# Issuing the reloads of the weight buffers from GpSimd's queue instead of SyncE's in a hybrid mLSTM/HGRN2 layer

## The chip, the cores and the metric

The kernel runs on one core of a Trainium2 chip. The metric is the device time of one execution in microseconds (us), lower is better. The core has five engines that each run their own list of instructions in order: TensorE (PE: matmuls; its weight loads are shown as PEld), VectorE (DVE), ScalarE (ACT), GpSimd (POOL) and SyncE (SP), which here does nothing but start transfers (DMAs). A transfer is started by an instruction of one engine's list, is carried out by 16 DMA engines, and raises a semaphore when it has landed.

## The reference

One inference step of one decoder layer for 320 tokens: 256 of a new prompt, and 8 sequences of 8 sample tokens. All is float32, D = 2048. One input projection `proj = x @ w_in` feeds two token mixers and two merge gates. Mixer A is an mLSTM with 4 heads (keys of 256, values of 512), mixer B an HGRN2 recurrence with 8 heads (128 and 256). Then:

```python
ya = branch_a @ w_branch_a          # branch_a = norm(mLSTM(q, k, v)) * sigmoid(o)
yb = branch_b @ w_branch_b          # branch_b = norm(HGRN2(q, f, i)) * silu(g)
merged = sigmoid(gate_a) * ya + sigmoid(gate_b) * yb
x1 = layernorm(alpha * x + merged @ w_out)
y  = layernorm(alpha * x1 + square(relu(x1 @ w_up)) @ w_down)
```

Besides y, the new states of both mixers are returned (C, n, m of the mLSTM and S of HGRN2), for the prompt and for each of the 8 sample sequences.

## The kernel before

**The work on weights.** All weight matrices together are 304 tiles of 2048 x 128. A tile is multiplied in 16 steps along its 2048 rows, and each step takes three matmuls of 128 x 128 by 128 x 320: since one matmul of the fast float32 kind doesn't keep all bits, weights and tokens are split into a high and a low part (`wh`, `wl`; `xh`, `xl`), and high x high, high x low and low x high are summed in one PSUM bank. That makes 304 x 16 x 3 = 14592 matmuls, and PE runs them in the order of the tiles: for each of 4 mLSTM heads four tiles of values, two of keys, two of queries and two of merge gates; four more gate tiles; for each of 8 HGRN heads two gate tiles and the head's four; then the output gates, the branch projections, `w_out`, and four rounds of `w_up` and `w_down`.

**How weights come.** Weights move in units of half a tile: 128 x 1024 float32, 512 KB, 608 units, numbered in the order of use. A unit goes through these steps:

1. a transfer from memory into one of three raw buffers (`self.wr`, `RAW` = 3, unit u in buffer u % 3). The first six units come in pieces (`start`, at the head of the program); each later one is a *reload* (`reload`, L511 to L513);
2. ACT copies raw to `wh` (`prep`, instruction at helper line L334, shown as `wh<-wr`);
3. DVE computes raw minus `wh`, which is `wl` (`low_half`, L504, shown as `wl<-wr,wh`). With that the raw buffer is free, and `low_half` of unit u starts the `reload` of unit u + 3;
4. PE uses the pair `wh`, `wl` in 24 matmuls, and gives it back (`give`). There are three such pairs; from the `w_out` tiles on five more, carved out of a buffer `bb`.

`A` (L334), `mm` (L340) and `dma` (L343) are helpers, so nearly all of ACT's operations, of the weight matmuls and of SP's transfers show the helper's line; they are told apart by the names of their tiles.

**The heads.** What the mLSTM and HGRN heads do with their projections runs beside the weight matmuls: small matmuls on PE between those on weights (L1117, L1316, and others at L340 such as `bank<-f`), evacuations of PSUM banks on ACT (`f<-bank`), and element work on DVE. Much of it is turned or copied by round trips through memory, all issued by SP: stores of a transposed head output in small pieces (`turned`, L1311 and L1322, shown as `hT<-f`; the pieces of the sample tokens leave from a pool of two small buffers), the values of a head turned once by a store into `vtD` and a load back (`rows_to` L1010, `rows_from` L1018), copies of the sample tokens' values (`copies_to` L1069, `copies_from` L1075, `vsDm`), and the keys, written once into `kD` (L1096, eight stores per head) for use at the end. The old states C are loaded (L1349) and the new ones stored by SP as well. At the end of the kernel `m_C` reads the keys and the turned values back for the prompt's new state C, by four pairs of loads issued by GpSimd (L1197, L1198). GpSimd has else only memsets: at the start, and during the HGRN heads at L1431, L1436 (which fills a buffer after DVE has read it at L1434) and once at L428.

**What sets the order.** The program is written out by a planner in Python (`Sched`, L145 to L232) when the kernel is built. It holds one modelled clock per engine (`pe`, `act`, `dve`, `pool`, `sp`). `run_main` walks through the weight matmuls, adds 147 ns to PE's clock for each, and after each step *pumps* the chains: generators which yield requests of the form (engine, cost in ns, function). A request is issued when its modelled inputs are ready at PE's modelled time or nearly so; that puts the instruction at the end of its engine's list. Chains with a lower priority number go first, and a reload has -1, the first of all. So the order on every engine follows from modelled costs, and the chip then runs each list in order, whatever the real times. For transfers the model adds fixed times to landing: a reload's data are ready for `prep` 3200 ns after its modelled issue ends (L513), a store of turned values 5000 ns after it.

Of the kernel before, what the change touches and what calls it, by code (L numbers as in the profile page):

```python
# [295 lines left out]
class Program:  # L296
# [212 lines left out]
            self.rest_ev.t = e  # L509

    def reload(self, u, at):  # L511
        t = yield ("sp", 620, lambda: self.dma(self.wr[:, u % self.RAW, :], self.d["wt"][u]), (at,))
        self.raw_at[u] = t + 3200.0  # L513

    def run_main(self):
# [1720 lines left out]
```

## Time and profile before

| | us |
|---|---|
| median of 3 runs | 2289.7 |
| lowest and highest of these | 2287.66 and 2290.4 |
| the profiled execution, its time | 2291.95 |
| the profiled execution, its span | 2290.2 |
| TensorE's mean granted clock in it (share of full) | 0.998 |

The profiled execution is one run recorded instruction by instruction. Its span goes from the first recorded instruction to the last; the time of the execution holds 1.75 us around it. DMA moved 432.88 MB in the span, 189 GB/s, of which the hardware queue used by SP had 427.24 MB and the software queue used by GpSimd 3.15 MB.

How to read the lines: in the page's part on engines, a name is followed by its busy time, its share of the span and its number of instructions. In the part on groups, a line names the source line, the engine, the operation and output<-input by the program's names, then the count, the busy time and the mean time of one in ns, and behind the second bar the idle time just before these instructions and what ended it. In a timeline a row begins with the start and the duration in us, and a bracket holds the idle time before it and what it waited for. In a list of waits the columns are the total, the number and the longest. A queue's own row has the engine's name with a q (SPq).

### The profile page before, as it was taken

What the parts mean: (1) busy time and instruction counts of PE and PEld (TensorE: products, weight loads), DVE (VectorE), ACT (ScalarE), POOL (GpSimd) and SP (SyncE); (2) the same over time, 40 slices, a digit from 0 to 9 for tenths busy, and PEclk for the clock granted to TensorE, in tenths of its full rate; (3) what the DMA queues carried; (4) which work ended last, traced back from release to release, by engine and by line L of the source; (5) the groups of instructions that cost most, each with busy time, mean ns of one, the idle gap of its engine ahead of it and who ended that gap; (6) DMA issues with size and microseconds to landing.
All of it is one profiled execution on the core that took longest, in us unless ns stands there. A gap on an engine that the chain in (4) does not pass through costs nothing.

```text
span 2290.2 us, 39073 instructions
## 1 busy us (share of the span) xinstructions
PE 2272.9 (99%) x15546; PEld 2234.0 (98%) x15546; DVE 1425.1 (62%) x2490; ACT 1013.0 (44%) x1574; POOL 13.5 (1%) x42
## 2 busy tenths in 40 slices
PE   9999999999999999999999999999999999999998
PEld 8999889999999999999999999999999999999998
DVE  6667568788888876555655769544444444444566
ACT  5443445455555565444433547423433343334434
POOL 0000000000000000000000000000000000000000
PEclk9999999999999999999999999999999999999999
DMA  7898697676777665555555644444444444444644
GB/s 234 277 280 283 215 287 232 212 222 202 215 220 231 198 199 174 172 172 177 175 170 190 213 153 145 155 149 152 151 147 150 154 148 148 152 151 148 197 153 157
DMA packets 251167, 432.88 MB, mean 189 GB/s; under 512 B 106844, under 2 KB 146916, under 8 KB 250984
## 3 DMA queue, kind: packets, MB, share of 16 engines
q1 hardware_dynamic: 250088, 427.24, 57.7%
q0 software_dynamic: 896, 3.15, 0.5%
q8 instruction: 122, 2.00, 0.4%
q14 instruction: 61, 0.50, 0.1%
HBM read 377.30 MB, written 53.00 MB: 188 GB/s over the span
## 4 chain that ended last, share of the span: by engine, by line
PE 91%; DMA 4%; DVE 2%; ACT 1%; SPq 1%; issue 1%; ACTq 0%; DVEq 0%
PE bank L340 91%; DMA wr<-wt 3%; ACT wh L334 1%; DVE wl L504 1%; SPq L343 1%; ACT f3m L334 0%; DMA f<-xT 0%; DMA f2a<-scr 0%; DMA scr<-f 0%; DMA hT<-f 0%; DMA rx<-wt 0%; DVE rx L1378 0%; ACT f L334 0%; ACT oC L334 0%; DVE f L1007 0%
## 5 line engine op out<-in xcount | busy, mean ns | idle before, releaser
L340 PE MATMUL bank<-xh,wh 128*128 128x320 f32 x2408 | 760.3, 317 | 0.4 <-ACT wh L334 0.4
L340 PE MATMUL bank<-xh,wl 128*128 128x320 f32 x2408 | 744.1, 310 | 0.1
L340 PE MATMUL bank<-xl,wh 128*128 128x320 f32 x2408 | 741.2, 309 | 0.0
L334 ACT ACTIVATE wh<-wr 128x1024 fp32r<-128x1024 f32 (+1 forms) x432 | 453.0, 1049 | 642.5 <-PE bank L340 561.3
L504 DVE TENSOR_TENSOR wl<-wr,wh 128x1024 fp32r<-128x1024 f32 x423 | 516.9, 1222 | 333.5 <-ACT wh L334 325.4
L340 PEld LDWEIGHTS bank<-xh,wh 128*128 128x128 f32 x2408 | 453.5, 189 | 6.7 <-issue 3.9
L340 PEld LDWEIGHTS bank<-xl,wh 128*128 128x128 f32 x2408 | 453.2, 188 | 2.7
L340 PEld LDWEIGHTS bank<-xh,wl 128*128 128x128 f32 x2408 | 453.7, 189 | 0.6 <-DVE wl L504 0.6
L334 ACT ACTIVATE bb<-wr 128x1024 fp32r<-128x1024 f32 x181 | 191.9, 1061 | 356.4 <-PE bank L340 342.2
L504 DVE TENSOR_TENSOR bb<-wr,bb 128x1024 fp32r<-128x1024 f32 x179 | 219.1, 1225 | 162.3 <-ACT bb L334 162.3
L340 PE MATMUL bank<-xh,bb 128*128 128x320 f32 (+1 forms) x1280 | 284.1, 309 | 0.0
L340 PE MATMUL bank<-ra,bb 128*128 128x320 f32 x1264 | 283.4, 308 | 0.0
L340 PE MATMUL bank<-rxb,bb 128*128 128x320 f32 x1112 | 255.0, 309 | 0.0
L340 PE MATMUL bank<-ra,wh 128*128 128x320 f32 x892 | 248.9, 308 | 0.0
L340 PEld LDWEIGHTS bank<-xh,bb 128*128 128x128 f32 x1280 | 214.7, 188 | 0.0
L340 PEld LDWEIGHTS bank<-ra,bb 128*128 128x128 f32 x1264 | 210.6, 188 | 0.2
L340 PE MATMUL bank<-xl,bb 128*128 128x320 f32 (+1 forms) x640 | 197.5, 309 | 0.0
L340 PEld LDWEIGHTS bank<-rxb,bb 128*128 128x128 f32 x1112 | 188.4, 188 | 0.2
L340 PE MATMUL bank<-rxb,wl 128*128 128x320 f32 x596 | 183.7, 308 | 0.0
L340 PE MATMUL bank<-rxb,wh 128*128 128x320 f32 x596 | 183.7, 308 | 0.0
L340 PEld LDWEIGHTS bank<-ra,wh 128*128 128x128 f32 x892 | 161.4, 188 | 0.0
L340 PEld LDWEIGHTS bank<-xl,bb 128*128 128x128 f32 x640 | 120.2, 188 | 0.0
(333 smaller groups left out, 2145.3 us busy)
## 6 DMA issues: line engine op xcount, KB each, us to landing
wr<-wt SPq DMA_DIRECT2D x602, 512.0 KB
rx<-C SPq DMA_DIRECT2D x34, 256.0 KB
Cs<-rx SPq DMA_DIRECT2D x34, 256.0 KB
f<-C SPq DMA_DIRECT2D x30, 256.0 KB
Cs<-f SPq DMA_DIRECT2D x30, 256.0 KB
f<-xT SPq DMA_DIRECT2D x26, 160.0 KB
f<-S SPq DMA_DIRECT2D x8, 512.0 KB
f3h<-S SPq DMA_DIRECT2D x8, 512.0 KB
```

Source lines behind the costliest of these rows:

```text
L334: return self.nc.scalar.activation(out, in_, func, **kw)
L340: self.nc.tensor.matmul(*a, **kw)
L343: self.nc.sync.dma_start(out, in_)
L504: self.V().tensor_tensor(lo, raw, hi.bitcast(F32), ALU.subtract)
```

## The change

One line of `reload` is changed. The transfer is requested from the engine `pool` and issued by `self.nc.gpsimd.dma_start`, where it was requested from `sp` and issued by the helper `dma`, which is `self.nc.sync.dma_start`. The cost that the planner counts is 1000 in place of 620. The 602 reloads of units 6 to 607 are concerned; the transfers of the first six units, in `start`, stay on SP, and so do all transfers of the heads.

```diff
     def reload(self, u, at):
-        t = yield ("sp", 620, lambda: self.dma(self.wr[:, u % self.RAW, :], self.d["wt"][u]), (at,))
+        t = yield ("pool", 1000, lambda: self.nc.gpsimd.dma_start(self.wr[:, u % self.RAW, :], self.d["wt"][u]), (at,))
         self.raw_at[u] = t + 3200.0
```

As the planner decides with its clocks, all five lists are written anew: SP's loses the 602 reloads, GpSimd's gains them, and the order on PE, ACT and DVE differs from that of before in about the first 825 us of the program.

## The prediction

> **What bounds the kernel now.** I read the page's first line, then a table of windows, then the waits and the timelines of the windows in which TensorE stood. The columns of the windows are the stretch, its length, the busy time of PE, PEld, DVE, ACT and POOL (with counts), TensorE's granted clock, the DMA engines' busy share and GB/s.
>
> ```profile
> PE 2272.9 (99%) x15546; PEld 2234.0 (98%) x15546; DVE 1425.1 (62%) x2490; ACT 1013.0 (44%) x1574; POOL 13.5 (1%) x42
> ```
> ```profile
> 40.00:150.00 110.00, 109.83 (x749) 103.70 (x748) 69.89 (x144) 44.60 (x75) 0.00 (x0) 1.00 0.87 276
> 150.00:243.00 93.00, 88.71 (x602) 82.55 (x601) 60.40 (x119) 38.28 (x67) 0.00 (x0) 1.00 0.87 272
> 243.00:250.00 7.00, 6.31 (x27) 5.87 (x27) 3.63 (x9) 1.82 (x5) 0.00 (x0) 0.51 0.54 170
> 250.00:400.00 150.00, 147.53 (x1007) 136.66 (x1007) 106.78 (x210) 66.84 (x113) 0.00 (x0) 1.00 0.77 246
> 400.00:825.00 425.00, 425.00 (x3012) 416.96 (x3011) 349.55 (x893) 225.50 (x457) 4.28 (x17) 1.00 0.71 215
> 825.00:2200.00 1375.00, 1375.00 (x9376) 1374.68 (x9375) 752.90 (x985) 574.76 (x753) 0.00 (x0) 1.00 0.49 163
> ```
>
> TensorE is the bound: busy for 99% of the span, and for every recorded microsecond from 400 to 2200 us. There a faster weight transfer can bring nothing. One matmul takes 1375.00 / 9376 = 147 ns there, so the 24 matmuls that use one unit of weights (half a tile, 512 KB) take 24 × 147 ns = 3.53 us. What can be gained lies between 40 and 400 us: PE's idle time is 0.17 + 4.29 + 0.69 + 2.47 = 7.6 us, and in 243 to 250 us the clock stood at 0.51, which costs 6.31 × 0.49 = 3.1 us more. So the **ceiling of any gain is 10.7 us**, 0.47% of the span. The last 90 us hold reloads for three units only and I give them nothing.
>
> Who ended those waits? PE's waits of 40 to 400 us (total, times, longest) and PE's timeline, with the wait in brackets:
>
> ```profile
> PE bank L340 <- ACT f L334: 4.6, 3, 2.3
> PE bank L1117 <- DVE f2a L1059: 2.4, 3, 0.8
> PE bank L340 <- ACT ra L334: 0.4, 1, 0.4
> ```
> ```profile
> 154.82 0.48 PE L340 MATMUL bank<-f 128*128 128x256 f32 x1 [0.71 <-ACT f L334]
> 158.56 0.33 PE L1117 MATMUL bank<-cst,f2a 128*128 128x128 f32 x1 [0.83 <-DVE f2a L1059]
> 166.29 0.38 PE L340 MATMUL bank<-misc,f 128*128 128x1 f32 x2 [0.45 <-ACT ra L334]
> 241.70 0.48 PE L340 MATMUL bank<-f 128*128 128x256 f32 x1 [2.30 <-ACT f L334]
> 245.32 0.47 PE L1117 MATMUL bank<-cst,f2a 128*128 128x128 f32 x1 [0.69 <-DVE f2a L1059]
> 329.69 0.48 PE L340 MATMUL bank<-f 128*128 128x256 f32 x1 [1.62 <-ACT f L334]
> 333.43 0.33 PE L1117 MATMUL bank<-cst,f2a 128*128 128x128 f32 x1 [0.84 <-DVE f2a L1059]
> ```
>
> No weight matmul waits. PE stands at a head's own matmuls, in mLSTM heads 1 (2.0 us), 2 (3.0 us, and the 3.1 us of clock) and 3 (2.5 us), because ACT and DVE delivered the head's operands late. Why was ACT late? Head 3 shows it on SyncE (SP), DVE and ACT:
>
> ```profile
> 319.87 1.90 SPq L343 DMA_DIRECT2D wr<-wt  x1
> 321.87 0.91 SPq L343 DMA_DIRECT2D hT<-f  x2
> 322.87 0.60 SPq L343 DMA_DIRECT2D kD<-f2a  x1
> 323.52 0.55 SPq L343 DMA_DIRECT2D hT<-f  x1
> 324.13 0.64 SPq L343 DMA_DIRECT2D kD<-f2a  x1
> 324.87 1.83 SPq L343 DMA_DIRECT2D wr<-wt  x1
> ```
> ```profile
> 315.02 1.23 DVE L504 TENSOR_TENSOR wl<-wr,wh 128x1024 fp32r<-128x1024 f32 x1 [2.47 <-ACT wh L334]
> 320.17 1.23 DVE L504 TENSOR_TENSOR wl<-wr,wh 128x1024 fp32r<-128x1024 f32 x1 [2.84 <-ACT wh L334]
> ```
> ```profile
> 327.31 1.06 ACT L334 ACTIVATE wh<-wr 128x1024 fp32r<-128x1024 f32 x1 [4.92 <-DMA wr<-wt]
> 329.22 0.42 ACT L334 ACTIVATE f<-bank 128x320 f32<-128x320 f32 x1
> 329.93 1.06 ACT L334 ACTIVATE wh<-wr 128x1024 fp32r<-128x1024 f32 x1 [0.28 <-DMA wr<-wt]
> ```
>
> DVE ended with a raw buffer at 315.02 + 1.23 = 316.25; the reload of that buffer was issued at 319.87, 3.6 us later, because small stores of hT and kD stood ahead of it in SP's order. The next one: 321.40 to 324.87, 3.5 us. ACT runs in order: it waited 4.92 us for the first of these weights, and the evacuation `f<-bank` for which PE stood (to 329.69) came behind it, at 329.22. Weights late by SP's queue, not by the wire, are what holds head 3; head 1 has the same form. From 40 to 400 us ACT waits for weights 50 us in all:
>
> ```profile
> ACT wh L334 <- DMA wr<-wt: 50.1, 19, 4.9
> ```
>
> Head 2 is another case, in ACT's timeline:
>
> ```profile
> 239.09 0.22 ACT L334 ACTIVATE f<-bank 128x64 f32<-128x64 f32 x1 [5.70 <-DMA hT<-f]
> ```
>
> Here ACT waited 5.70 us for a store of hT to land, as the two small buffers out of which those stores read were both in flight.
>
> **The change part by part.** *Removed from SP:* the reloads, 602 issues on the page:
>
> ```profile
> wr<-wt SPq DMA_DIRECT2D x602, 512.0 KB
> ```
>
> In the jam above one reload held SP for 1.90 or 1.83 us, a small store for 0.45 to 0.64 us. What stays there (hT, kD, vtD, vsDm, C) comes up earlier by the reloads that stood ahead of it.
>
> *Added to GpSimd:* 602 issues. The transfers that GpSimd already issues at the end of the kernel give a price (median us from issue to landing; then busy time and mean ns):
>
> ```profile
> bb<-vtD POOLq DMA_DIRECT2D x2, 512.0 KB, 5.0
> wr<-vtD POOLq DMA_DIRECT2D x2, 512.0 KB, 6.3
> ```
> ```profile
> L1198 POOL DMA_DIRECT2D bb<-vtD x2 | 1.8, 899 | 11.8 <-DVE f3m L2091 10.1 <-PE bank L340 1.7
> L334 ACT ACTIVATE wh<-wr 128x1024 fp32r<-128x1024 f32 (+1 forms) x432 | 453.0, 1049 | 642.5 <-PE bank L340 561.3
> L504 DVE TENSOR_TENSOR wl<-wr,wh 128x1024 fp32r<-128x1024 f32 x423 | 516.9, 1222 | 333.5 <-ACT wh L334 325.4
> ```
>
> An issue takes 0.90 us of GpSimd, once in 3.53 us, on an engine that is busy for 13.5 us in all. A raw buffer goes round once in three units, 3 × 3.53 = 10.6 us. ACT's copy takes 1.05 and DVE's subtraction 1.22 us of that, and I estimate 0.2 us for semaphores, so a transfer may take **8.1 us from its release to its landing** before PE waits for weights. The rows say 5.0 and 6.3 us for 512 KB: hidden, with 1.8 us left in the worse one. Bounds: at 5.0 to 6.3 us nothing is lost; at the spread's next step of the same size, 7.6 us, still nothing. I take nothing, and keep the other end as a rival.
>
> *Wait added:* GpSimd runs in order too, so a memset in front of a reload holds it. In a row of GpSimd's timeline:
>
> ```profile
> 453.34 0.37 POOL L1436 MEMSET f<- 128x320 f32 x1 [39.85 <-DVE f L1434]
> ```
>
> Such a memset (L1431, L1436, and L428 once) belongs to a head of the HGRN branch and waits for DVE at L1434. The comparison of the two instruction orders puts each behind a reload and in front of another. Queued behind it are only reloads, and for these ACT waits. Its price lies between nothing and the wait for DVE's line minus the 1.8 to 3.1 us of slack; DVE is 349.55 / 425 = 82% busy there, and 0.37 us is the memset itself. I take nothing. Near the end the four L1197/L1198 loads come ahead of the last three reloads; these are needed later than those loads were issued, so nothing.
>
> *Moved:* the planner counts a reload as ready 3.2 us after its modelled issue, on the engine that it now finds empty, so the whole program is planned anew until about 825 us. By the comparison of orders, a head's own matmuls on PE come 24 to 33 weight matmuls (3.5 to 4.9 us) earlier than before in heads 0 to 3; ACT's and DVE's operations for them move ahead likewise. If they keep pace, nothing; if not, PE waits for up to that much at each place.
>
> *Sum.* Heads 1 and 3: their weights are no longer behind SP's stores, and ACT gets to the evacuations in time: −2.0 − 2.5 = −4.5 us. Head 2: SP loses the reloads in its jam, six of them, of which the first and the last were
>
> ```profile
> 223.46 0.40 SPq L343 DMA_DIRECT2D wr<-wt  x1
> ...
> 241.55 0.35 SPq L343 DMA_DIRECT2D wr<-wt  x1
> ```
>
> or some 2.4 us at 0.40 us each, against the 5.70 us for which ACT waited; but the new order also puts the buffers' next use one unit (3.5 us) earlier. I take half of its 3.0 + 3.1 = 6.1 us, −3.0 us (bounds: 0 and −6.1). Together −7.5 us. The profiled execution took 2291.95 us, its span was 2290.2 us; it becomes 2284.4. The median of the runs shown is 2289.7 us, 2.2 us lower, and becomes **2282 us**.
>
> One rule weighs against this. The Trainium skill, page "DMA: Bandwidth & Descriptors", section "Issuing engines are not separate DMA queues", says that transfers started by different engines end on the same 16 DMA engines and interleave there, so that a second issuing engine saves only the sequencer's time. By that rule no byte moves faster, and the sum would be only what SP's order costs. The trace agrees that DMA is well used (0.87 in the first two windows), but also shows that it is the order on SP that costs: 3.6 and 3.5 us of the waits above went by ahead of the issue.
>
> **The rivals.**
>
> *A. All stalls go.* Head 2 is cured too, since SP's jam of stores is shorter, and its clock stays up. For it: SP's issues are fewer by 602. Against it: landing of the hT stores is untouched and only two buffers serve them. −10.7: 2279 us.
>
> *B. No change.* The wait moves from SP's queue to the DMA engines, 0.87 busy until 243 us: the reload is issued 3.5 us earlier and lands hardly earlier, as the small stores' packets now compete with it; or head 2 and the new order eat what heads 1 and 3 give. For it: 0.87, and 512 KB in 3.53 us are 149 of the 276 GB/s there. Against it: the time lost in head 3 went by ahead of the issue. About 2288 to 2291.
>
> *C. Slower by the new order.* The matmuls of a head stand 3.5 to 4.9 us earlier in PE's order, but what ACT and DVE bring for them depends on round trips through memory (hT, kD, vtD) whose landing the planner assumes at fixed times. It decides from the point at which those chains, waiting for landings that didn't get faster, gain less than 3.5 us: then PE stands 3.5 us longer at each of heads 1, 2 and 3, and one place in head 0 or in the HGRN heads, +14 us: 2304 us, less the 4.5 us that the earlier weights still bring, 2299 us. For it: DMA at 0.87. Against it: the evacuations were held by late weights, not by those landings, in two of three heads.
>
> *D. Slower by software transfers.* It decides above 8.1 us from release to landing: each unit of PE's then takes a third of the excess. At 8.4 us, 0.1 us × 602 = +60 us. For it: 6.3 us in the slower row, in a stretch where DMA is only half busy. Against it: both rows lie below, and DMA is at 0.49 for 1375 us. Confined to the windows at 0.87 (200 us, 57 units), it would be +6 us: 2296.
>
> **How the numbers follow.** A measurement of this kernel can tell about 0.2%, 4.6 us, from no change; so faster means below 2285.1, slower above 2294.3. Forecast (heads 1 and 3, half of head 2; 2279.5 to 2284.5): 0.40. A: 0.20. B: 0.17. C: 0.15. D: 0.08, two thirds of it the confined case. Faster: 0.40 + 0.20 = 0.60, and 0.02 of B. Slower: 0.15 + 0.08 = 0.23, less 0.02 for weak cases of C. Same: 0.17. The range must leave out no more than 0.2: below, A's 2279 with 1 us of scatter, 2278; above, all of B and the confined D, and the weaker half of C, 2297.
>
> **What would show it.** Right: PE's brackets at heads 1 and 3 gone, L512's reloads on POOL landing 5 to 6.5 us after issue, ACT's wait for `wr<-wt` (50 us there before) down, windows from 400 us still full. Head 2 right: the wait for `hT<-f` on ACT shorter but there, the clock's dip in one window smaller. Wrong: new brackets at L1117 or at `bank<-f` in head 0 or the HGRN heads (C); PE waiting for `wl` or `wh`, and ACT for `wr<-wt`, beyond 400 us (D); reloads that take as much longer to land as they are issued earlier (B).

## The result and the profile after

The changed kernel takes 2305.34 us (median of 6 runs, 2304.68 to 2306.83), against 2288.52 us for the kernel before (6 runs on the same chips): a ratio of 1.0074, 95% interval 1.0061 to 1.0087. **It is slower by 17 us**, where 2282 us and a range up to 2297 were forecast. The profiled executions, 2304.68 against 2291.95 us, lie 12.7 us apart, since the one of before is slower than each of its six runs (2286.4 to 2290.4 us) and the one after is the fastest of its own; lines of the two are compared below, and times by their medians.

The windows of the changed kernel (columns as before):

```profile
0.00:40.00 40.00, 35.39 (x226) 31.15 (x227) 26.28 (x48) 22.54 (x44) 5.78 (x22) 0.96 0.71 235
40.00:150.00 110.00, 110.00 (x756) 104.71 (x755) 74.07 (x151) 45.70 (x77) 14.34 (x27) 1.00 0.86 279
150.00:243.00 93.00, 88.74 (x597) 83.06 (x595) 55.51 (x112) 32.97 (x58) 10.62 (x20) 0.98 0.82 255
243.00:250.00 7.00, 0.00 (x0) 0.00 (x0) 3.04 (x7) 4.54 (x11) 0.33 (x1) 0.73 0.65 140
250.00:400.00 150.00, 144.89 (x973) 134.36 (x974) 103.83 (x209) 62.66 (x106) 18.25 (x35) 0.98 0.75 238
400.00:825.00 425.00, 423.52 (x3001) 415.03 (x3000) 348.42 (x886) 222.73 (x454) 61.01 (x124) 1.00 0.71 216
825.00:2200.00 1375.00, 1375.00 (x9377) 1374.67 (x9376) 752.70 (x983) 577.36 (x760) 210.34 (x396) 1.00 0.50 163
```

From 825 to 2200 us PE is full, as before: the steady state has lost nothing. Between 40 and 400 us PE is idle for 4.26 + 7.00 + 5.11 = 16.4 us (7.6 before), and a clock of 0.98 in two windows costs (88.74 + 144.89) × 0.02 = 4.7 us (3.1 before). 400 to 825 us adds 1.5 us. New is also the loss in the first window, at a clock of 0.96, which in the kernel before was

```profile
0.00:40.00 40.00, 37.88 (x253) 34.00 (x254) 29.18 (x55) 23.79 (x46) 2.70 (x17) 1.00 0.74 241
```

PE's longest waits from 0 to 400 us, and their rows in its timeline:

```profile
PE bank L1117 <- DVE f2a L1059: 16.4, 3, 8.1
PE bank L340 <- DMA f<-xT: 3.3, 1, 3.3
```
```profile
24.03 1.06 PE L340 MATMUL bank<-f 128*32 128x320 f32 x4 [3.29 <-DMA f<-xT]
157.67 0.48 PE L1117 MATMUL bank<-cst,f2a 128*128 128x128 f32 x1 [3.23 <-DVE f2a L1059]
250.12 0.47 PE L1117 MATMUL bank<-cst,f2a 128*128 128x128 f32 x1 [8.14 <-DVE f2a L1059]
339.00 0.47 PE L1117 MATMUL bank<-cst,f2a 128*128 128x128 f32 x1 [4.99 <-DVE f2a L1059]
```

In the kernel before, the first of these rows was

```profile
21.62 0.73 PE L340 MATMUL bank<-f 128*32 128x320 f32 x4 [0.76 <-DMA f<-xT]
```

PE stands once in each of heads 1, 2 and 3, and no longer at `bank<-f` but at L1117, whose operand DVE makes at L1059. What held DVE? ACT's timeline has the same three places:

```profile
154.61 1.06 ACT L334 ACTIVATE ra<-ra 128x1024 fp32r<-128x1024 f32 x1 [5.77 <-DMA ra<-vtD]
155.57 1.04 ACT L334 ACTIVATE wh<-wr 128x1024 fp32r<-128x1024 f32 x1
156.51 0.29 ACT L334 ACTIVATE f2a<-f2a 128x128 fp32r<-128x128 f32 x1
...
244.72 0.22 ACT L334 ACTIVATE f<-bank 128x64 f32<-128x64 f32 x1 [12.48 <-DMA hT<-f]
244.84 1.05 ACT L334 ACTIVATE ra<-ra 128x1024 fp32r<-128x1024 f32 x1
...
336.14 1.06 ACT L334 ACTIVATE ra<-ra 128x1024 fp32r<-128x1024 f32 x1 [7.73 <-DMA ra<-vtD]
```

In heads 1 and 3 ACT stands at `ra<-ra`, the split of the turned values, until their load from vtD has landed; in head 2 for 12.48 us at a small tail buffer of hT. Behind it in ACT's order are the next weights and `f2a<-f2a`, the high half of the operand for which PE stands. In the kernel before, ACT did its `ra<-ra` in heads 1 and 3 without a wait, at 153.40 and 328.28 us. The issues of the load on SP's queue, in heads 1 and 3 of the changed kernel, and in head 1 of the kernel before with its split on ACT:

```profile
148.86 0.50 SPq L343 DMA_DIRECT2D ra<-vtD  x1
328.89 0.95 SPq L343 DMA_DIRECT2D ra<-vtD  x1
```
```profile
144.69 0.49 SPq L343 DMA_DIRECT2D ra<-vtD  x1
153.40 1.04 ACT L334 ACTIVATE ra<-ra 128x1024 fp32r<-128x1024 f32 x1
```

In head 1 it landed 154.61 − 148.86 = 5.75 us later at most, between the 5.0 and 6.3 us that GpSimd's loads of the same values took in the kernel before; in head 3 it took 336.14 − 328.89 = 7.25 us at most, 0.9 us more than the slower of these. So the length of the load explains little of the waits of 5.77 and 7.73 us. Before, ACT came to the split 8.7 us after the load's issue; after the change it stood there at 154.61 − 5.77 = 148.84 us, as the load was just being issued, and the planner had counted 10 us between the two (`rows_from`). ACT came to it too soon. The reloads themselves do what the prediction said (source line L512, then the DMA list with size in KB and median us to landing):

```profile
L512 POOL DMA_DIRECT2D wr<-wt x602 | 319.9, 531 | 1900.2 <-DVE wl L504 965.2
```
```profile
wr<-wt POOLq DMA_DIRECT2D x602, 512.0 KB, 3.7
```

3.7 us is well under the 8.1 us that a unit has. ACT's wait for weights from 40 to 400 us fell from 50.1 to 4.7 us:

```profile
ACT ra L334 <- DMA ra<-vtD: 13.5, 2, 7.7
ACT f L334 <- DMA hT<-f: 13.2, 2, 12.5
...
ACT wh L334 <- DMA wr<-wt: 4.7, 3, 2.7
```

The weights are on time, and PE waits longer.

### The profile page after: what moved, and what is told of

Read it like the earlier page. It is cut to its first block, busy times and chain, and to the rows that moved or that the text cites. A ratio compares the mean times of both kernels' runs of the same rounds, so it can differ in the third digit from the quotient of the medians.

```text
span 2302.9 us, 39300 instructions
## 1 busy us (share of the span) xinstructions
PE 2273.8 (99%) x15546; PEld 2236.1 (97%) x15546; DVE 1427.9 (62%) x2490; ACT 1011.5 (44%) x1574; POOL 333.6 (14%) x644
## 4 chain that ended last, share of the span: by engine, by line
PE 94%; DMA 2%; issue 1%; SPq 1%; ACT 1%; DVE 1%; POOL 0%; ACTq 0%; POOLq 0%
PE bank L340 94%; SPq L343 1%; DMA wr<-wt 1%; DMA ra<-vtD 1%; DMA f<-xT 0%; ACT f3m L334 0%; ACT wh L334 0%; DVE wl L504 0%; DMA rx<-wt 0%; DMA hT<-f 0%; PE bank L1117 0%; ACT oC L334 0%; POOL wr L512 0%; PE bank L1316 0%; PE bank L1041 0%
## 5 line engine op out<-in xcount | busy, mean ns | idle before, releaser
L512 POOL DMA_DIRECT2D wr<-wt x602 | 319.9, 531 | 1900.2 <-DVE wl L504 965.2
```

The costliest lines, as they stand in the source:

```text
L512: t = yield ("pool", 1000, lambda: self.nc.gpsimd.dma_start(self.wr[:, u % self.RAW, :], self.d["wt"][u]), (at,))
```

## The experiments

The change does three things at once: it moves transfers to another queue, it makes the planner write another order, and it lets the first three reloads overtake the first loads. **Theory 1:** the new order costs. **Theory 2:** the software queue costs, by contention or late landing. The first four runs take them apart; the planner's request and the issuing instruction are separate in the source, so either can be changed alone.

**The new order, issued by SP:**

```diff
-  ("pool", 1000, lambda: self.nc.gpsimd.dma_start(self.wr[...], self.d["wt"][u]), (at,))
+  ("pool", 1000, lambda: self.dma(self.wr[...], self.d["wt"][u]), (at,))
```

> The planner counts the reloads as after the change (GpSimd, 1000 ns), so PE, ACT and DVE run exactly the order of the changed kernel; but SyncE issues the reloads, as before. Theory 1 (the new order costs: ACT stands at the turned values and the small tail buffers before they have landed): 8 to 12 us above before, about 2299, with waits of PE at L1117 like the 16.4 us of the changed kernel, and the start as before. Theory 2 (the software queue costs: its transfers take bandwidth from SP's small stores, or land late): within 3 us of before, 2289.

Measured: 2305.98 us, ratio 1.0068 (1.0055 to 1.0081), 16.4 us above before where theory 1 said 8 to 12. A loss as large is there without a single reload on GpSimd. Its waits from 40 to 400 us, of PE and then of ACT:

```profile
PE bank L1117 <- DVE f2a L1059: 16.2, 4, 5.8
PE bank L340 <- DVE wl L504: 3.2, 6, 0.7
```
```profile
ACT wh L334 <- DMA wr<-wt: 60.7, 22, 5.6
ACT f L334 <- DMA hT<-f: 10.8, 6, 3.7
```

The 16 us at L1117 come back, and 3.2 us of PE waiting for `wl` on top. So this order loses without the software queue. But ACT stands for something else here: never for the load of the turned values, whose split comes at 153.98 us without a wait, but for weights that are late behind SP's stores (60.7 us against 4.7 in the changed kernel) and for hT. The run shows that the order has no room for a late operand on ACT; which operation is late in the changed kernel, it doesn't show. That theory 2 falls altogether rests on the next pair and on the fastest kernel below.

**The old order, issued by GpSimd**, all reloads, and with the first three left on SP:

```diff
-  ("sp", 620, lambda: self.dma(self.wr[...], self.d["wt"][u]), (at,))
+  ("sp", 620, lambda: self.nc.gpsimd.dma_start(self.wr[...], self.d["wt"][u]), (at,))
...
+  ("sp", 620, lambda: (self.nc.gpsimd.dma_start if u >= 3 * FIRST else self.dma)(self.wr[...], self.d["wt"][u]), (at,))
```

> The planner counts the reloads as before (SP, 620 ns), so PE, ACT and DVE run exactly the order of before; but GpSimd issues them. Theory 1 (order): the 4.5 us of heads 1 and 3 are gained, the 3.5 us at the start are lost, since GpSimd's first three reloads come before the last of the first loads: 2284 to 2289. Theory 2 (software queue): most of the change's 17 us is there, 2300 to 2305.

> As the one before, but the first three reloads (units 6 to 8) stay on SP, behind the small loads of the start. Theory 1 and the start's loss: 3 to 4 us under the kernel with all reloads on GpSimd in the old order, so 2281 to 2285. Theory 2: 2297 to 2302. If the start's loss is not due to these three transfers: equal to the run before.

Measured: 2287.56 us, ratio 0.9989 (0.9980 to 0.9998), and 2285.88 us, 0.9986 (0.9977 to 0.9995); before 2289.58 us. Both are a little faster than before, as theory 1 said (the second by 0.9 us less than its range), and nothing of the 2297 to 2305 us of theory 2 is there; the 1.7 us between them are inside their intervals, so this pair alone doesn't show the start's loss. Waits of the second from 40 to 400 us, PE and ACT:

```profile
PE bank L340 <- ACT f L334: 4.1, 1, 4.1
```
```profile
ACT f L334 <- DMA hT<-f: 9.9, 1, 9.9
ACT wh L334 <- DMA wr<-wt: 6.2, 3, 3.2
```

Here is the prediction's mechanism by itself. Heads 1 and 3 have no wait of PE any more. Head 2 has one of 4.1 us in place of 2.30 and 0.69, and ACT's wait for hT has grown from 5.70 to 9.9 us: with the reloads gone from SP's list, ACT reaches the tail buffer 5.8 us earlier (227.6 us in place of 233.4), and the store lands only 1.6 us earlier (237.48 in place of 239.09).

**The changed kernel with the first three reloads on SP**, its order on PE, ACT and DVE kept:

```diff
-  ("pool", 1000, lambda: self.nc.gpsimd.dma_start(self.wr[...], self.d["wt"][u]), (at,))
+  ("pool", 1000, lambda: (self.nc.gpsimd.dma_start if u >= 3 * FIRST else self.dma)(self.wr[...], self.d["wt"][u]), (at,))
```

> The changed kernel, its order on PE, ACT and DVE kept exactly, with the first three reloads on SP. Start theory (PE's 3.29 us wait for the last tokens, 0.76 before, comes from these three transfers on GpSimd's queue): 3 to 4 us under the changed kernel, about 2302. Rival (the start's loss is given back at the first head): 2305, as the changed kernel.

Measured: 2301.94 us, ratio 1.0054 (1.0041 to 1.0066), 3.4 us under the changed kernel by the medians (of two series of runs; the two intervals overlap). The trace shows where it comes from. The three reloads in the changed kernel, on GpSimd, and in the one before, on SP:

```profile
15.41 1.75 POOL L512 DMA_DIRECT2D wr<-wt  x3
```
```profile
20.82 2.10 SPq L343 DMA_DIRECT2D wr<-wt  x3
```

SP's order had kept them behind the last first loads. On their own queue they go 5.4 us sooner, 1.5 MB beside the last tokens, and PE's wait for the tokens is 3.29 us where it was 0.76. With the three on SP this wait is gone, and PE's first 40 us are full but for 1.00 us at the very start:

```profile
0.00:40.00 40.00, 39.00 (x257) 35.96 (x258) 30.14 (x55) 24.42 (x47) 4.72 (x20) 1.00 0.72 244
```

The Trainium skill, page "DMA: Bandwidth & Descriptors", section "Queues, rings and completion order", says that each DMA engine takes turns between the queue rows for which it has work, packet by packet. By that rule a transfer in another queue takes its share from one that was started before it; the 3.29 us agree. But overtaking alone doesn't always cost this. In the old order with all reloads on GpSimd, the three go as early, and PE waits for the tokens for only 0.27 us:

```profile
15.43 1.75 POOL L512 DMA_DIRECT2D wr<-wt  x3
```
```profile
21.88 0.73 PE L340 MATMUL bank<-f 128*32 128x320 f32 x4 [0.27 <-DMA f<-xT]
```

Why the tokens landed some 2 us later in the changed kernel is open, with one trace of each.

**What in the order costs?** The next three runs alter the planner's model in the kernel just told. First, the cost of SP's stores in small pieces; then, at the unchanged cost, the time at which the turned values are taken as landed; then also the time at which a tail buffer is taken as free. The 17 us of the second aren't how long that load takes (7.25 us at most above); they allow for an SP that runs behind the plan:

```diff
-  ("sp", 620, ...)      # stores to vtD, vsDm, kD, and hT at L1311
+  ("sp", 1000, ...)
...
-        yield from self.rows_from(self.vtD[h], vhl[:, 0], vhl[:, 1], 10000.0)
+        yield from self.rows_from(self.vtD[h], vhl[:, 0], vhl[:, 1], 17000.0)
...
     def back(self, pool, x):
-        yield wait(self.later(4000))
+        yield wait(self.later(12000))
```

> The changed kernel with the first three reloads on SP, and the planner counts 1000 ns in place of 620 for each store in small pieces on SP (turned values, sample copies, keys, hT). Theory (the planner thinks SP empty once the reloads are off it, and so puts operations that wait for SP's round trips too early on ACT): the plan spreads out again and most of PE's 19.6 us at L1117 goes; 2284 to 2291. Rival (no plan without the reloads on SP's modelled clock is good, since the landings themselves are later): 2298 or more.

> The changed kernel with the first three reloads on SP, and the planner counts the load of the turned values (vtD) as ready 17 us after its issue in place of 10, so that only ACT's split of these values moves back in ACT's order at first. Theory (in heads 1 and 3 ACT stands at that split, and behind it are the operations PE waits for): heads 1 and 3 give back 6.0 and 6.7 us, head 2 (small tail buffers) stays: 2289 to 2293. Rival (ACT would wait for something else in the same place): 2299 or more.

> As the one before, and the planner counts the two small tail buffers as free 12 us after the store's issue in place of 4. Theory: head 2 gives back its 7.0 us too: 2283 to 2287, at or under before. Rival (head 2's loss is not the tail buffers): equal to the run before.

Measured, against 2288.60 us before: 2281.53 (0.9966, 0.9952 to 0.9979), 2286.44 (0.9985, 0.9976 to 0.9994), and **2279.36 us (0.9958, 0.9945 to 0.9970)**. All three are faster than their expected ranges. Two numbers of the planner's model turn 12 us of loss into 9 us of gain. What PE still waits for from 40 to 400 us, in the second and the third of these:

```profile
PE bank L1117 <- DVE f2a L1059: 4.9, 1, 4.9
```
```profile
PE bank L340 <- DMA ra<-vsDm: 1.2, 1, 1.2
```

The second has its wait in head 2 alone; heads 1 and 3 are clean, as expected, and the run lies 2.6 us under the expected range. The third is clean in head 2 too, and has 1.2 us in head 1, at a load of vsDm.

Does the loss go because PE's matmul at L1117 is put later again, or because of the order on ACT? The traces tell. Counted up to heads 1, 2 and 3:

| | before | changed | fastest |
|---|---|---|---|
| weight matmuls on PE ahead of the first at L1117 | 819, 1296, 1779 | 792, 1272, 1752 | 786, 1266, 1746 |
| copies `wh<-wr` on ACT ahead of the split `ra<-ra` | 40, 60, 80 | 39, 58, 79 | 41, 60, 80 |
| copies `wh<-wr` on ACT ahead of `f2a<-f2a` | 41, 61, 81 | 40, 60, 80 | 39, 59, 79 |

In the fastest kernel the matmul stands on PE even 6 places earlier than in the changed one, and doesn't wait. On ACT the high half of its operand now comes ahead of the split, and not behind it. So the split of the turned values (heads 1 and 3) and the reuse of the tail buffers (head 2), placed ahead of that operand on ACT before their transfers have landed, are the cause. The first of the three runs, which names neither place and only counts SP's stores as longer, does nearly as well in another way: ACT still waits 11.7 us at the split, but PE's matmul comes only after 825, 1311 and 1803 weight matmuls, later than before the change.

**Four tail buffers in the old order**, another way to cure head 2:

```diff
         self.tst2 = B(320)
+        B = Part(self.f2, 2640)
+        self.tail.free += [(0.0, B(64)) for _ in range(2)]
```

> Reloads on GpSimd but for the first three, planner's costs as before the change, and four small tail buffers in place of two (the program is planned anew with them). Theory (the one wait that is left with the old order, 4.1 us at head 2, is ACT waiting for a tail buffer's store to land): it goes, 2280 to 2283. Rival (the new plan, or SP's jam, makes a wait elsewhere): 2286 or more.

Measured: 2285.20 us, ratio 0.9984 (0.9975 to 0.9992): a miss, equal to the old order with two buffers (0.9986). The store's wait halves, but ACT still stands in head 2, and PE with it:

```profile
PE bank L340 <- ACT f L334: 3.1, 1, 3.1
```
```profile
ACT f L334 <- DMA hT<-f: 4.7, 1, 4.7
```

More buffers shorten the wait and don't remove it; a later use of two, though in another order, did better.

**What is the queue worth in a good order?** Two runs on SP: the kernel before with the two times altered as in the fastest kernel, and the exact order of the fastest kernel.

```diff
# first: the kernel before, with 17000.0 and later(12000) as above
# second: the fastest kernel, with
-  ("pool", 1000, lambda: (self.nc.gpsimd.dma_start if u >= 3 * FIRST else self.dma)(self.wr[...], ...), (at,))
+  ("pool", 1000, lambda: self.dma(self.wr[...], ...), (at,))
```

> The kernel before (all reloads on SP, planned so), with only the planner's two landing times corrected: turned values ready 17 us after the load's issue, tail buffers free after 12 us. Theory (order and queue are two separate terms, the queue worth about 4 us in either order): head 2's wait goes, those of heads 1 and 3, which come from weights late behind SP's stores, stay in part: 2283 to 2286. Rival 1 (only the plan counts, the queue is worth nothing): 2279 to 2281. Rival 2 (late weights dominate): 2288 or more.

> Exactly the order on PE, ACT and DVE of the kernel with turned values and tails later (2279.4 us), with all reloads issued by SP. It measures the queue alone in a good order. Theory: 4 us over that kernel, 2283 to 2285, with ACT waiting for weights again (50 us and more from 40 to 400 us). Rival 1 (queue worth nothing): 2279 to 2281. Rival 2 (this order has no room for late weights, PE waits for wl and wh as in the first experiment): 2288 or more.

Measured, against 2288.91 us before: 2283.34 (0.9974, 0.9965 to 0.9983) and 2287.43 us (0.9994, 0.9985 to 1.0003). The first lies in its range, with 3.3 us of PE waiting at L1117 in heads 1 and 2; the second is 2.4 us over its range and 0.6 us under rival 2. In the second, PE's and ACT's waits from 40 to 400 us are

```profile
PE bank L1117 <- DVE f2a L1059: 2.1, 2, 1.5
PE bank L340 <- DVE wl L504: 1.3, 3, 0.7
PE bank L340 <- ACT f L334: 1.1, 1, 1.1
```
```profile
ACT wh L334 <- DMA wr<-wt: 53.8, 20, 4.9
```

against 3.1 us of waiting for weights in the fastest kernel. The table puts the orders against the queues, as ratios to before:

| order on PE, ACT, DVE | reloads on SP | on GpSimd but the first three | all on GpSimd |
|---|---|---|---|
| as before | 1 | 0.9986 | 0.9989 |
| as the change makes it | 1.0068 | 1.0054 | 1.0074 |
| with both times altered, planned for GpSimd | 0.9994 | 0.9958 | not run |
| with both times altered, planned for SP | 0.9974 | not run | not run |

From the first row to the second the order costs 0.7 to 0.85%. Along a row the queue gains 0.14% in the first two orders (in the first its interval excludes 1, in the second the intervals overlap) and 0.36%, 8 us, in the third, where the intervals lie apart. But the third order was planned for GpSimd. With each queue in the order planned for it, 0.9974 against 0.9958, the queue gains 0.16%, 3.7 us, and the intervals just overlap.

## Why the prediction was wrong

- **What bounds the kernel: right.** The gain and the loss lie in the first 400 us, but for 1.5 us up to 825 us; from 825 to 2200 us PE is full in both kernels. The ceiling of 10.7 us held: the best kernel gained 9.2.
- **Removed and added: right.** GpSimd's issue took 0.53 us, less than the 0.90 us that I took, the landing 3.7 us, less than 5.0. The 0.2 us for semaphores was an estimate for which no row was given: the changed kernel's trace has 0.08 to 0.10 us from a landing to ACT's copy, 0.03 us from its end to DVE's start, and 0.29 us from DVE's end to GpSimd's issue, 0.4 us in all, which leaves 7.9 us in place of 8.1. Memsets in front of reloads cost nothing that shows. With the old order heads 1 and 3 came clean; of the 4.5 us forecast for them the run kept 3.7 in all, head 2 being worse.
- **Head 2: wrong even in the old order.** "Some 2.4 us" less of SP's jam, half of 6.1 us gained: PE's wait there grew from 3.0 to 4.1 us, as ACT got there sooner and its wait for the store went from 5.70 to 9.9 us. The late weights had been hiding part of this wait.
- **Moved: the step that failed.** It was costed at nothing "if they keep pace", and this with no look at what keeps pace on ACT. In the changed kernel PE waited 16.4 us at L1117 in heads 1 to 3, because ACT stood at the split and at a tail buffer ahead of the operand; with these two put later on ACT, and the first three reloads on SP, the waits at L1117 were gone and the ratio to before fell from 1.0054 to 0.9958. Why the order came out so: the planner's own clock, with the reloads off its SP, has the issue of the load of the turned values end at 132.4, 213.3 and 298.4 us in heads 1, 2 and 3, where it had 135.9, 217.6 and 301.2 before the change. On the chip the same loads came 7, 23 and 17 weight matmuls later than before (after 756, 1240 and 1719, in place of 749, 1217 and 1702). The model moved them forward by 3 to 4 us and the chip back by 1 to 3 us.
- **Rival C** had the place and the form, and gave it 14 us, less 4.5; I gave it 0.15. Its reason was only half of it: the matmuls did stand earlier on PE, but in the fastest kernel they stand earlier still. I had compared the places of PE's operands and their makers in the two orders, and not what stands ahead of the makers on ACT.
- **The start: missed.** Nothing in the prediction spoke of SP's order as a thing that holds the first three reloads back until the first loads are through. PE's wait and the clock there cost 3.29 − 0.76 = 2.5 us and 0.04 × 35.39 = 1.4 us in the changed kernel; in the old order the same three early reloads cost nothing clear of the noise.
- **The sum again:** order +16.4 (2305.98 − 2289.58), queue −4.0 (2301.94 − 2305.98), start +3.4 (2305.34 − 2301.94). These are steps from one run to the next, so that they add up proves nothing; the intervals of the last two steps overlap. And the terms aren't independent: with the reloads on SP the order loses by late weights, with the reloads on GpSimd by the split and the tail buffer.
- **The rule of the Trainium skill** against the change (page "DMA: Bandwidth & Descriptors", section "Issuing engines are not separate DMA queues"), that a second issuing engine only saves the sequencer's time: the runs agree as far as time in SP's list is what was gained. That time was worth 3.7 us in the old order and 3.7 to 8 us in the good ones, since the two reloads shown stood 3.6 and 3.5 us in SP's order, about as long as the 3.7 us that one takes to land. "Usually small relative to the DMA itself", as that section has it, isn't so for a transfer that stands behind a list of small stores.
- **What stays open:** why SP's own jam is no shorter without the reloads. Single stores hold SP for up to 3.9 us in the changed kernel, in these rows of head 2, where before none of hT's held it over 2.46 us and none of vtD's over 0.93:

```profile
221.98 5.80 SPq L343 DMA_DIRECT2D vtD<-f  x4
227.83 3.89 SPq L343 DMA_DIRECT2D hT<-f  x1
```

That the reloads, now running beside them, fill the DMA engines is likely and not shown. With the same order and all reloads on SP the longest vtD store held SP for 0.77 us, against 3.95 in the changed kernel and 2.61 with the first three reloads on SP, which speaks for it; for hT the three numbers are 2.79, 3.89 and 2.15, which doesn't.

## What to carry to other kernels

When a program's order is written out from modelled costs, moving work off an engine changes the model's clock for that engine and with it every order: try the queue and the order apart before judging either. Look on each in-order engine for the instruction that waits for a transfer, and for what stands behind it; an operand made late elsewhere may have hidden that wait. And a shared in-order queue is also a priority: what is moved to a queue of its own overtakes what used to be ahead of it, and may take time from it.

## What the runs showed of the hardware

GpSimd's 602 transfers of 512 KB in the changed kernel landed 3.7 us after the issue began at the median, 3.3 at least and 10.9 at most, and an issue took 0.53 us of GpSimd. How long SP's take to land the traces don't say, so the two can't be compared. SP's issue of a store in small pieces isn't a fixed cost: 0.32 to 3.89 us for the stores to hT, of 32 and 64 KB, in the changed kernel. And a long stall costs more than its idle time: the windows of the changed kernel with PE's waits of 3.2 to 8.1 us have a granted clock under 1.00 (0.96 in the first, 0.98, 0.73 and 0.98 between 150 and 400 us). The low clock comes behind the wait: the 3.29 us end at 24.03 us, and the clock is 0.58 and 0.57 in the two windows of 2 us from 24 to 28 us, in which PE is busy. Shorter waits left it at 1.00: 1.5 us in all from 400 to 825 us, and 2.8 us in all, none over 0.9, from 40 to 150 us of the first experiment.
